# An encoder layer on one core: the gate's SiLU, the gate's load and the first block sums moved

## The chip, the core and the metric

The kernel runs on one core of a Trainium2 chip. The metric is the device time of one execution in microseconds (us); lower is better. The core has a matrix engine (TensorE, in the profile PE, its weight loads PEld), a vector engine (VectorE, DVE), a scalar engine (ScalarE, ACT), a general engine (GpSimd, POOL) and a queue engine (SyncE, SP). Each works through its own instructions strictly in the order in which the program issued them, so an instruction that waits holds up all that stand behind it on its engine. Transfers are issued from SP and POOL and run on 16 DMA engines.

## The reference, cut to what matters

One layer over 512 tokens of width 2048:

```python
h = rmsnorm(x); proj = h @ w_in                      # 2048 x 6176
aq, ak, av, gq, gk, gv, gr, glr = split(proj)
attn_out = mixture_of_dilations(aq, ak, av)          # 16 heads of 64
o = gla(forward) + gla(backward)                     # 4 heads, gated linear attention
gla_out = rmsnorm_per_head(o) * gla_norm_w * silu(gr)
x = x + concat(attn_out, gla_out) @ w_out
h = rmsnorm(x)
x = x + (silu(h @ w_gate) * (h @ w_up)) @ w_down     # hidden width 5632
out = rmsnorm(x)
```

`gr` (width 1024) is the output gate of the gated linear attention ("GLA"): its SiLU is taken early, kept in DRAM, and multiplied in at the end of each GLA head.

## The kernel before

All products work on float32 values split into a rounded part (`hi`, made by ACT) and a remainder (`lo`, made by DVE), and each product is hi x hi + hi x lo + lo x hi. Most large products use a fast scheme with seven instead of eight block products of 2 x 2 blocks; its weight operands are four raw blocks and four sums of them ("block sums", class `Blocks`, `sums`, lines 1394 to 1396), and its results are put together by an evacuation (`evac7`).

The program is written out by hand in one order; there is no planner. These parts matter here.

**The front stage (`Front.run`).** Twelve units of 256 output columns, four weight pieces each: units 0 to 3 are the output gate `gr`, units 4 to 11 are q and k of the windowed attention. For piece i the loop issues the splits and sums of the next pieces (`split(i + 1)`, lines 1407 and 1412; `sums(i + 2)`), then the 14 pairs of products (lines 1489 and 1503), then one call of `run_urgent`, which takes one step of the oldest pending generator. At the last piece of a unit, `evac7` starts: its first step copies and adds the seven PSUM results (lines 1523 and 1529 to 1537). Its second step, one piece later, makes the last add (line 1523, 128 x 512) and issues four accumulating DMAs on POOL (lines 1548 to 1551) that add three partial results into the unit's output tile. Three empty steps follow, the third of which ends in `finish`: DVE multiplies by the row scale (line 1646), and for a gate unit ACT takes SiLU (line 1650) and POOL stores both halves to DRAM (`grd`, line 1651), all in one step. With one step a piece, the multiplication and SiLU of unit u fall at the end of piece 3 of unit u + 1, behind that unit's own first evacuation step.

**Side work.** After the front stage, attention and the four GLA heads run as generators beside the projections. Each half weight piece of a projection earns credit, and each step of side work costs one. `gla(h)` loads its gate (`load_gate`, line 877, issued on POOL) just before the step that transposes the normalized output (line 1093) and multiplies it by the gate (line 1096). Line 966 makes the decayed q and k, line 998 multiplies them on PE; `load_gv` loads the values.

**Block sums made ahead (`Feed.ahead`).** The feed-forward's gate and up projections (`Feed`, 44 units of four pieces) need DVE for block sums. For 21 pieces, those of `pre`, the sums are made earlier, during the projections of the mixed output: raw blocks are loaded by SP, four adds are made in place (line 1463), and POOL stores them to DRAM (`sd`, line 1465). Later `Feed.sums` loads them on SP. The pace is set by `j.ahead`, steps a half piece, for the six projections before the last. The first five pieces' sums are made directly from the raw blocks, in six smaller instructions a piece (`halves=True`), during the last two projections (`before_out`, called at pieces 5, 7, 9, 11 and 13 of their 16 halves). Their splits (line 1412) stand on DVE among the remainders of the projection's own weights (line 218).

## Time and profile before

| | |
|---|---|
| median of three executions | 2179.76 us (2178.83 to 2181.34) |
| the profiled execution | 2178.09 us, span 2176.3 us |
| PE busy | 2156.1 us (99%) |
| DVE busy | 1821.7 us (84%) |
| ACT busy | 1221.7 us (56%) |
| POOL busy | 359.8 us (17%) |
| front stage, row-scale multiplications of its 12 units | 143.9 to 379.4 us |
| block sums made ahead | 624.6 to 821.1 us |
| products of gate and up begin | 850.8 us |

How to read the rows: a row of the timeline has its start, its duration, engine, source line (L1646 is line 1646), operation, the tiles written and read (a and b are the two pools of buffers, ps is PSUM), the shape, and in square brackets how long the engine had stood idle before it and what ended that wait. A row of the view of stretches has the stretch, its length, then the busy time and the number of instructions of PE, PEld, DVE, ACT and POOL, the granted clock of PE as a share of full speed, the busy share of the DMA engines, and GB/s. "DMA to landing" is the time from a DMA's issue to its completion.

### The profile page before, as it was taken

The numbers are of one execution on the slowest core, as the hardware profiler recorded it, in microseconds if no ns is written. First come the engines' busy times: TensorE is split into PE (matmuls) and PEld (weight loads), VectorE is DVE, ScalarE is ACT, GpSimd is POOL, SyncE is SP. The second block draws the span as 40 slices with busy tenths as digits, with TensorE's granted clock in tenths as the row PEclk, the third lists the DMA queues.
The fourth block names the chain that finished last, engine by engine and source line by source line (L and its number), as shares of the span: only waits on it lengthen the run. The fifth ranks groups of instructions, "written<-read, shape, count | busy, mean of one in ns | idle before, by whom it ended". The sixth has DMA issues, their size and how long they took to land.

```text
span 2176.3 us, 34923 instructions
## 1 busy us (share of the span) xinstructions
PE 2156.1 (99%) x12682; PEld 1899.3 (87%) x12682; DVE 1821.7 (84%) x3153; ACT 1221.7 (56%) x2229; POOL 359.8 (17%) x503
## 2 busy tenths in 40 slices
PE   9999999999999999999999999999999999999998
PEld 7888887888887888988888888888888899999987
DVE  6698996777768678899899999998999888898885
ACT  8455554677655445555555555555555655555562
POOL 0012123211011110012211122121221220021300
PEclk9999999999999999999999999999999999999999
DMA  6467779536366773377767677677777985576982
GB/s 201 141 174 173 174 179 251 165 120 187 109 224 212 251 261 117 122 182 178 197 178 182 181 177 196 177 181 184 177 193 174 269 204 173 184 183 156 284 309 78
DMA packets 264475, 405.71 MB, mean 186 GB/s; under 512 B 19373, under 2 KB 163421, under 8 KB 264302
## 3 DMA queue, kind: packets, MB, share of 16 engines
q1 hardware_dynamic: 205502, 272.49, 39.6%
q0 software_dynamic: 58480, 130.45, 26.7%
q8 instruction: 100, 1.64, 0.3%
q14 instruction: 73, 0.60, 0.1%
q10 hardware_dynamic: 320, 0.53, 0.1%
HBM read 287.47 MB, written 66.39 MB: 163 GB/s over the span
## 4 chain that ended last, share of the span: by engine, by line
PE 57%; DVE 0%; DMA 0%; issue 0%; ACT 0%; DVEq 0%; ACTq 0%
PE ps L1503 24%; PE ps L1489 12%; PE ps L1867 5%; PE ps L1868 5%; PE ps L1866 5%; PE ps L348 1%; PE ps L346 1%; PE ps L347 1%; PE ps L2063 1%; PE ps L2061 1%; PE ps L2062 1%; DMA gd<-b 0%; DVE b L1412 0%; DVE a L2094 0%; DVE a L1523 0%
## 5 line engine op out<-in xcount | busy, mean ns | idle before, releaser
L1407 ACT CAST b<-b 128x768 fp32r<-128x768 f32 (+1 forms) x569 | 518.7, 944 | 373.4 <-DVE b L1412 181.7
L1412 DVE TENSOR_TENSOR b<-b,b 128x768 fp32r<-128x768 f32 (+1 forms) x569 | 597.8, 1085 | 36.4 <-ACT b L1407 25.2
L1503 PE MATMUL ps<-b,b 128*128 128x512 f32 x1656 | 484.3, 393 | 0.9 <-ACT b L1407 0.7
L1503 PE MATMUL ps<-a,b 128*128 128x512 f32 x1368 | 401.4, 394 | 2.1 <-DVE b L1523 1.7
L1503 PEld LDWEIGHTS ps<-b,b 128*128 128x128 f32 x1656 | 280.8, 188 | 32.8 <-ACT b L1407 1.5
L1489 PEld LDWEIGHTS ps<-b,b 128*128 128x128 f32 x1656 | 271.3, 190 | 39.3
L1489 PE MATMUL ps<-b,b 128*128 128x256 f32 x1656 | 296.8, 280 | 0.0
L1489 PEld LDWEIGHTS ps<-a,b 128*128 128x128 f32 x1368 | 227.0, 189 | 38.1 <-DVE b L1412 2.1
L1503 PEld LDWEIGHTS ps<-a,b 128*128 128x128 f32 x1368 | 228.0, 189 | 25.6 <-ACT b L1407 2.5
L1489 PE MATMUL ps<-a,b 128*128 128x256 f32 x1368 | 246.0, 281 | 0.5 <-DVE b L1412 0.2
L1394 DVE TENSOR_TENSOR b<-b 128x512 f32<-128x512 f32 x260 | 178.3, 686 | 21.7 <-DMA b<-in_w_down_dram 6.4
L1866 PE MATMUL ps<-b,b 128*128 128x256 f32 x624 | 176.6, 283 | 0.0
L1867 PE MATMUL ps<-b,b 128*128 128x256 f32 x624 | 176.6, 283 | 0.0
L1868 PE MATMUL ps<-b,b 128*128 128x256 f32 x624 | 176.6, 283 | 0.0
L1866 PEld LDWEIGHTS ps<-b,b 128*128 128x128 f32 x624 | 119.8, 192 | 0.0
L1867 PEld LDWEIGHTS ps<-b,b 128*128 128x128 f32 x624 | 119.8, 192 | 0.0
L1868 PEld LDWEIGHTS ps<-b,b 128*128 128x128 f32 x624 | 119.8, 192 | 0.0
L1396 DVE TENSOR_TENSOR b<-b,b 128x256 f32<-128x256 f32 x260 | 110.7, 426 | 8.9
L1395 DVE TENSOR_TENSOR b<-b,b 128x256 f32<-128x256 f32 x260 | 110.5, 425 | 9.0
L346 PE MATMUL ps<-b,b 128*128 128x512 f32 x292 | 117.0, 401 | 0.3 <-ACT b L455 0.3
L348 PE MATMUL ps<-b,b 128*128 128x512 f32 x292 | 114.1, 391 | 0.2 <-DVE b L459 0.2
L347 PE MATMUL ps<-b,b 128*128 128x512 f32 x292 | 113.9, 390 | 0.0
(301 smaller groups left out, 4199.3 us busy)
## 6 DMA issues: line engine op xcount, KB each, us to landing
b<-in_w_gate_dram SPq DMA_DIRECT2D x109, 512.0 KB, 4.0
b<-in_w_up_dram SPq DMA_DIRECT2D x88, 512.0 KB, 4.4
b<-in_w_down_dram SPq DMA_DIRECT2D x88, 512.0 KB, 5.5
b<-a POOLq DMA_DIRECT2D x162, 256.0 KB, 4.6
b<-in_w_in_dram SPq DMA_DIRECT2D x78, 512.0 KB, 3.9
b<-in_w_out_dram SPq DMA_DIRECT2D x32, 512.0 KB, 5.3
gd<-b POOLq DMA_DIRECT2D x22, 512.0 KB, 4.0
b<-gd SPq DMA_DIRECT2D x22, 512.0 KB, 5.5
```

What stands on the lines that cost most here:

```text
L346: mm(o, xh.t[:, c], wh.t[:, w], start=first and not on, stop=False, skip_group_check=on)
L347: mm(o, xh.t[:, c], wl.t[:, w], start=False, stop=False, skip_group_check=on)
L348: mm(o, xl.t[:, c], wh.t[:, w], start=False, stop=last, skip_group_check=on)
L1394: dve.tensor_tensor(s_[:, :, 0:2], r[:, :, 1:3], r[:, :, 0:1].to_broadcast(shape), op=OP.add)
L1396: dve.tensor_tensor(s_[:, :, 3], s_[:, :, 2], r[:, :, 3], op=OP.add)
L1407: act.copy(o, src)
L1412: dve.tensor_tensor(o, src, h, op=OP.subtract)
L1489: mm(o, wl, xh, start=False, stop=end, skip_group_check=True)
L1503: mm(o.rearrange("p (s t) -> p s t", s=2), wh, x_, start=first and p == 0, stop=False, skip_group_check=True)
L1866: mm(o, xh[:, t], wh, start=first and h == 0, stop=False, skip_group_check=True)
L1867: mm(o, xh[:, t], wl, start=False, stop=False, skip_group_check=True)
L1868: mm(o, xl[:, t], wh, start=False, stop=last, skip_group_check=True)
```

## The change

1. **Front stage.** For gate units the generator's last part is cut in two: the multiplication in one step, SiLU and the store (one DMA instead of two) in the next. To make room, `Front.run` calls `run_urgent` twice in piece 0 of units 1 to 4.
2. **GLA.** One step more behind the products of line 966; the gate is loaded behind the first state products instead of just before it is used, and a step stands where the load was.
3. **Block sums.** The first five pieces of gate and up join `pre` (26 instead of 21); their sums are loaded from DRAM as two halves each, at the places where they were computed. The pace of `ahead` rises from 1.25 to 1.5 steps a half piece for the first three projections, from 2.0 to 2.25 for the next two and from 1.0 to 2.25 for the one after them.

```diff
@@ gla(h) @@
             if h % 2 == 0:
                 load_gv(h // 2)
             yield
+            yield
             put(gq.pop(h), gk.pop(h))
...
             sums(0)
+            load_gate(h)
             yield
             decays(0)
             sums(1)
...
             put(*os_)
-            load_gate(h)
+            yield
             yield
@@ Feed.__init__ @@
                 self.pre = {i: n for n, i in enumerate(
-                    i for i, (u, q) in enumerate(seq) if u > 1 and q == 1 and u % 2 == 0)}
+                    i for i, (u, q) in enumerate(seq) if i < 5 or u > 1 and q == 1 and u % 2 == 0)}
@@ Feed.sums @@
                     self.n_sums += 1
-                    S = s4.get(F32, self.shape(4))
-                    self.S[i] = [S]
-                    sp.dma_start(out=S.t.rearrange("p a b c -> p (a b c)"), in_=self.sd[self.pre[i]])
+                    n = 2 if halves else 1
+                    S = [s2.get(F32, [P, 1, 4, P]) for _ in range(2)] if halves else [s4.get(F32, self.shape(4))]
+                    self.S[i] = S
+                    for p, S in enumerate(S):
+                        sp.dma_start(out=S.t.rearrange("p a b c -> p (a b c)"),
+                                     in_=self.sd[self.pre[i]][:, p * 1024 // n:(p + 1) * 1024 // n])
@@ Front.finish @@
                     dve.tensor_tensor(c_.t, c_.t, rb[1].t[:, None, :].to_broadcast([P, 2, 512]), op=OP.mult)
-                    if u < 4:
-                        tables(SILU)
-                        for f in (1, 0):
-                            act.activation(c_.t[:, f], c_.t[:, f], AF.Silu, scale=1.0 - 2.0 * f)
-                            pool.dma_start(out=grd[u][:, f * 512:(f + 1) * 512], in_=c_.t[:, f])
-                    else:
+                    if u >= 4:
                         pool.dma_start(out=qkd[u - 4], in_=c)
+                        put(c_)
+
+                if u < 4:
+                    do()
+                    yield
+                    tables(SILU)
+                    for f in (1, 0):
+                        act.activation(c_.t[:, f], c_.t[:, f], AF.Silu, scale=1.0 - 2.0 * f)
+                    pool.dma_start(out=grd[u], in_=c)
                     put(c_)
-
-                if u == len(self.units) - 1:
+                elif u == len(self.units) - 1:
                     self.late = do
@@ Front.run @@
                     run_urgent()
+                    if q == 0 and 0 < u <= 4:
+                        run_urgent()
                     if done:
                         urgent.append(done)
@@ the order of the jobs @@
-            j.ahead = {n_out: 0.0, n_out - 1: 1.0}.get(n, 2.0 if n_in <= n < n_out else 1.25 if n_in - 3 <= n < n_in else 0.0)
+            j.ahead = {n_out: 0.0, n_in: 2.25}.get(n, 2.25 if n_in < n < n_out else 1.5 if n_in - 3 <= n < n_in else 0.0)
```

More of the change, by code (lines that the diff above doesn't have):

```diff
@@ L2133, in layer @@
             if n == n_out:
-                assert next(state["sums"], None) is None
+                assert next(state["sums"], 0) == 0
                 ff.run()
```

## The prediction

> **What bounds the kernel now.** I read the page first, then the waits, then the places that the waits name.

> ```profile
> PE 2156.1 (99%) x12682; PEld 1899.3 (87%) x12682; DVE 1821.7 (84%) x3153; ACT 1221.7 (56%) x2229; POOL 359.8 (17%) x503
> ```

> TensorE (PE) is busy for 99% of the span, so a change pays only where PE stands still, and costs only where it makes PE stand still. The view of the waits, PE's rows alone, says who keeps it (us in total, times, longest):

> ```profile
> PE ps L347 <- DVE a L218: 2.0, 1, 2.0
> PE ps L1503 <- DVE b L1523: 1.9, 5, 1.0
> PE ps L998 <- DVE a L1096: 1.8, 1, 1.8
> PE ps L1093 <- ACT b L1086: 1.5, 2, 1.1
> PE ps L1503 <- ACT b L1407: 1.1, 5, 0.2
> ```

> Three places, one for each part of the change: the entry to the feed-forward (L347), the front stage with its gate units (L1503), the gated attention (L998, L1093). The edits cannot win more than these stops and the slow clock after them.

> **Part 1, the front stage.** In the timeline of VectorE (DVE), L1523 over 128x512 is the add that opens a unit's last step; right behind it POOL issues that unit's four accumulating DMAs. L1646 is the multiplication by the row scale, which reads what those DMAs wrote.

> ```profile
> 128.23 0.69 DVE L1523 TENSOR_TENSOR b<-b,a 128x512 f32<-128x512 f32 x1
> ...
> 149.43 0.69 DVE L1523 TENSOR_TENSOR b<-b,a 128x512 f32<-128x512 f32 x1
> ...
> 157.08 0.69 DVE L1394 TENSOR_TENSOR b<-b 128x512 f32<-128x512 f32 x1
> ...
> 162.19 0.76 DVE L1523 TENSOR_TENSOR a<-ps,a 128x256 f32<-128x256 f32 x2 [0.19 <-DMA b<-a]
> ...
> 163.65 1.22 DVE L1646 TENSOR_TENSOR b<-b,a 128x1024 f32<-128x1024 f32 x1
> ...
> 166.81 2.18 DVE L1412 TENSOR_TENSOR b<-b,b 128x768 fp32r<-128x768 f32 x2 [0.42 <-ACT b L1407]
> ...
> 168.90 0.69 DVE L1523 TENSOR_TENSOR b<-b,a 128x512 f32<-128x512 f32 x1
> ...
> 171.43 0.69 DVE L1394 TENSOR_TENSOR b<-b 128x512 f32<-128x512 f32 x1 [1.84 <-issue]
> ...
> 190.32 0.69 DVE L1523 TENSOR_TENSOR b<-b,a 128x512 f32<-128x512 f32 x1
> ...
> 211.72 0.69 DVE L1523 TENSOR_TENSOR b<-b,a 128x512 f32<-128x512 f32 x1
> ```

> From add to add one unit passes. 149.43 to 168.90 is 19.47; less the two idle times in it (0.19 and 0.42) DVE needs 18.86. PE needs as much: the stretch of an undisturbed unit without gate is 19.52.

> ```profile
> 248.58:268.10 19.52, 19.52 (x113) 17.14 (x114) 18.26 (x31) 9.96 (x17) 4.07 (x5) 1.00 0.68 162
> ```

> So DVE has 0.7 us to spare in a unit, and the four gate units (128.23 to 211.72, 83.49) run above that. The cause shows on ScalarE (ACT):

> ```profile
> 186.32 1.15 ACT L1650 ACTIVATE b<-b 128x512 f32<-128x512 f32 x2 [3.00 <-DVE b L1646]
> ```

> SiLU waits 3.00 for the multiplication, ACT's roundings behind it come late, the store of the gate comes late, and DVE then waits 1.84 for the buffer that the store reads.

> Now count the steps. Each unit's evacuation is a generator, one step a weight piece; the multiplication is its fifth. Before, the steps fall on the next unit's pieces 0, 1, 2, 3 after the first. The change calls twice in piece 0 for the gate units, so steps two and three fall on piece 0, four on piece 1, the multiplication on piece 2, SiLU on piece 3. SiLU keeps its piece; the multiplication moves one piece forward. In DVE's queue its new place is before the block sums at 157.08, that is 157.08 - 149.43 = 7.65 after the add. Has the data landed by then? POOL's timeline, and the landing times of L1551 and L1549 over the four gate units (min/median/max):

> ```profile
> 136.76 1.20 POOL L1551 DMA_DIRECT2D b<-a  x1
> ...
> 157.78 0.86 POOL L1550 DMA_DIRECT2D b<-a  x1 [5.30 <-DMA b<-a]
> 158.32 1.20 POOL L1551 DMA_DIRECT2D b<-a  x1
> ...
> 177.95 1.21 POOL L1551 DMA_DIRECT2D b<-a  x1
> ...
> 200.00 1.20 POOL L1551 DMA_DIRECT2D b<-a  x1
> ```
> ```profile
> DMA to landing us min/median/max: 3.7/3.8/5.6
> ```
> ```profile
> DMA to landing us min/median/max: 5.6/6.2/6.8
> ```

> No. The third DMA waits for the first two, which overlap it; the fourth is issued 8.53, 8.89, 9.05 and 9.68 after the add, and lands 3.7 to 5.6 later (the four landings sum to 3.7 + 2 x 3.8 + 5.6 = 16.9). The times from add to landing sum to 36.15 + 16.9 = 53.05, on average 13.3 against 7.65. DVE stands about 5.6 us in each unit; queued behind the multiplication are the sums and remainders of the next unit's first piece, then the evacuation that frees PSUM, and PE waits for both. In the old place, 163.65 - 149.43 = 14.2 after the add, the data are there.

> After the landing DVE still has 18.86 - 7.65 = 11.21 of its unit to do. Four units take 53.05 + 4 x 11.21 = 97.9 instead of 83.5: **+14.4**. PE and ACT are no cover: PE finishes the unit in 19.5, within 24. The gains are already in this: the 1.84 and 0.42 are not in the 18.86, and a late gate buffer would be waited for inside the landing time. Ends: with the shortest landing (3.7) four times, 36.15 + 14.8 + 44.84 - 83.49 = +12.3; if PE alone set the pace, 4 x 19.52 - 83.49 = -5.4. I take the sum of the four, measured at this very place, with +18 (another 1 us a unit, the spread of L1549) as upper end. One store of 512 KB for two of 256 KB saves POOL an issue; POOL stands idle behind it, so nothing.

> [...]

> **Part 2, gated attention.** One yield more behind the products with q and k, one more behind the scaling, and the gate's load (L877, POOL) eight steps sooner. PE, timeline:

> ```profile
> 657.67 1.86 PE L1093 MATMUL ps<-idn,b 128*128 128x128 f32 x8 [1.06 <-ACT b L1086]
> 660.06 1.05 PE L998 MATMUL ps<-a,a 128*128 128x128 f32 x8
> ...
> 689.65 1.49 PE L1093 MATMUL ps<-idn,b 128*128 128x128 f32 x8 [0.45 <-ACT b L1086]
> 693.61 0.60 PE L998 MATMUL ps<-a,a 128*128 128x128 f32 x3 [1.77 <-DVE a L1096]
> ```

> Then the idle time that ended at the gate's landing (view of L1096), the gate load's time to landing (view of L877), and the first and last product of L998:

> ```profile
>   DMA b<-grd: 14.6, 3
> ```
> ```profile
> DMA to landing us min/median/max: 6.4/9.2/10.7
> ```
> ```profile
> L998 PE MATMUL ps<-a,a x64: 270/275/377, 629.2 to 721.3; 128*128 128x128 f32 x64
> ```

> Eight 128-wide products take 1.05 when fed. The transposes lose 1.06 + 0.81 and 0.45 + 0.44 because their scaling was issued just ahead of them; a step between them removes that. The 1.77 come from L1096, which stood for the gate, 14.6 us in three waits. The load lands 6.4 to 10.7 after its issue; one head's steps from its first L998 (629.2) to its transposes (657.67) are twelve in 28 us, so eight steps are some 19 us and cover it. Sum **-4.5**; ends -4.5 and +1 (a buffer of 4 KB a partition held 19 us longer, eight steps more of side work for the same credit; DVE, at 31.91 of 50 us in the row below, has room for a later crowd). On POOL the load passes the next head's loads and a store of block sums that waits for DVE; it can at worst stand behind such a store, where it stands today.

> **Part 3, entry to the feed-forward.** Stretches (us, PE, PEld, DVE, ACT, POOL, granted clock), then DVE's timeline:

> ```profile
> 845.00:848.20 3.20, 1.25 (x5) 1.05 (x6) 3.20 (x6) 0.00 (x0) 0.00 (x0) 1.00 0.07 10
> 848.20:851.60 3.40, 3.40 (x11) 2.80 (x10) 3.16 (x6) 1.95 (x6) 1.62 (x3) 0.50 0.67 218
> ```
> ```profile
> 835.23 0.42 DVE L1394 TENSOR_TENSOR a<-b 128x256 f32<-128x256 f32 x1
> ...
> 837.21 0.69 DVE L218 TENSOR_TENSOR a<-b,a 128x512 fp32r<-128x512 f32 x1
> ...
> 846.21 0.69 DVE L218 TENSOR_TENSOR a<-b,a 128x512 fp32r<-128x512 f32 x1
> ```

> PE stands 1.95 for the weight remainder at 846.21, and then runs 3.40 at a clock of 0.50, which costs 1.70. DVE has no gap in this stretch, and one piece's block sums, six instructions, hold it for 1.98 (835.23 to 837.21). Three of the five pieces lie in this last projection, two of them from 835 on: at least 4.0 us leave the queue ahead of a remainder that comes 1.95 late. **-3.65**, ends 0 and -3.65. What would be late next is the same remainder, 2 us later than needed to hurt.

> The price of it: 20 adds made ahead over the six projections before (L1463), which are 20 x 0.42 = 8.4 us of DVE in stretches like this one:

> ```profile
> L1463 DVE TENSOR_TENSOR b<-b x84: 410/419/428, 624.6 to 821.1; 128x256 f32<-128x256 f32 x84
> 700.00:750.00 50.00, 50.00 (x244) 42.26 (x244) 31.91 (x70) 23.82 (x63) 6.40 (x12) 1.00 0.66 220
> ```

> DVE is busy 31.91 of 50 there, so nothing; uncovered, where the rate more than doubles (1.0 to 2.25 a half piece, the last projection but one), it would be 8 adds, 3.4 us, less the two pieces of sums that leave that same projection, 4.0. SP issues five raw loads and ten loads of half sums more, POOL five stores more: 7.9 MB at the 220 GB/s of that row are 36 us of DMA time within 230, beside a share of 0.66. No weight load ends a wait of PE today; I take nothing, with +1 as end.

> **Sum.** 14.4 - 4.5 - 3.65 = **+6.25**. The profiled execution took 2178.09 (span 2176.3 and 1.8 around it), 1.67 under the median of the runs, 2179.76; on the median that is **2186.0**.

> **Rivals.** *Stall, but no gains* (the side steps meet new waits, the sums come late by DMA): 2179.8 + 14.4 = 2194. Against it: three waits with names, each taken apart from its cause. For it: 1.0 to 2.25 crowds DVE. A variant: each PE stop of some 4 us in the front is followed by 3.40 at half clock, as at 848; 4 x 1.70 = 6.8 more, 2193, if PE had no slack. It has: 19.5 + 1.7 against 24.5 a unit.

> *The accumulations land sooner* (other side, not slower). The first two need 5.6 to 6.8 while the last needs 3.7; the gate's store now leaves 3 us earlier and may no longer share the queue with them. It decides where 4 x (L + 11.21) - 83.49 = 8.15, an average L of 11.7 instead of 13.3. If the first two landed in 3.7 too, L = 13.3 - 2.5 = 10.8: front +4.5, total -3.6, 2176. Against it: 128.23 has no store ahead of it, and its L is the longest (8.53 + 5.6).

> *No stall at all* (faster): the data are there 7.65 after the add. Then DVE needs 18.86 and PE's 19.52 sets the pace: front -5.4, total -13.6, 2166. The rows have no L under 12. [...]

> **How the numbers follow.** Forecast 0.67, own range 2182 to 2191; stall without gains 0.10; sooner landings 0.15; no stall 0.08. Two runs of this kernel can be told apart from about 0.2%, 4.4 us: 2175.4 and 2184.1. Of the forecast 0.15 falls below 2184.1, of the sooner landings 0.05 below 2175.4. Slower 0.52 + 0.10 = 0.62, within 0.15 + 0.10 = 0.25, faster 0.05 + 0.08 = 0.13. The range, 2174 to 2194, leaves out the last rival, half of the first and the tails, 0.18.

> **What would show it.** Right: L1646 of the four gate units stands 3 to 6.5 us for a DMA of tile b, adds about 24 apart, PE waits of 2 to 4 us on DVE L1412 or L1523 between 140 and 230; no wait of L1650 for L1646; no idle time of L1096 for the gate; clock 1.00 at 848. Wrong: gate units at 21.4 or less, L1646 without idle time, or the L347 wait still there.

## The result, and the profile after

The changed kernel takes 2199.28 us (2197.20 to 2201.22), beside 2178.83 for the kernel before on the same chip: a ratio of 1.0092, 95% interval 1.0078 to 1.0107. Slower was right; 2186.0 was 13.3 us too low, and the range (2174 to 2194) did not hold the time.

TensorE's waits after the change, line numbers now those of the changed kernel (L1494 and L1508 are the old L1489 and L1503, L1414 the old L1412, L1528 the old L1523, L1284 the old L1282):

```profile
span 2199.5 us, 34945 instructions
PE 2165.2 (98%) x12682; PEld 1907.7 (87%) x12682; DVE 1820.5 (83%) x3143; ACT 1222.5 (56%) x2229; POOL 359.8 (16%) x504
...
PE ps L1494 <- DVE b L1414: 9.9, 5, 3.0
PE ps L1508 <- DVE a L1528: 3.6, 4, 1.0
PE ps L346 <- ACT a L237: 3.1, 1, 3.1
PE ps L1072 <- DVE b L1284: 2.5, 1, 2.5
PE ps L1508 <- DVE b L1528: 1.9, 3, 1.0
PE ps L1024 <- DVE b L1284: 1.6, 1, 1.6
```

The old waits that the prediction named are gone or shorter: L347's fell from 2.0 to 0.4, L998's for the gate and L1093's for the scaling are not there. In their place stand others, one kind for each part. Both kernels issue the same 12682 matmuls, so the delay can be read by number (the two profiled executions lie 23.2 apart, the medians 20.5): the start of the n-th matmul in one trace less that in the other (us, worked out from the two traces, at the matmul that starts nearest to each time of the kernel before).

```
                                        after less before
front stage, up to 206 us                    +20.0
rest of it, up to 234                         -1.0
on to 640 us                                  +0.4
gated attention, 640 to 760                   +1.5
entry to the feed-forward, up to 852          +1.8
after it                                      +0.4
sum (spans: 2199.5 - 2176.3 = 23.2)          +23.1
```

The three parts in turn. **Front stage**, DVE's timeline: the adds that open a unit's last step, and the multiplication (L1651):

```profile
128.13 0.68 DVE L1528 TENSOR_TENSOR b<-b,a 128x512 f32<-128x512 f32 x1
142.16 1.23 DVE L1651 TENSOR_TENSOR b<-b,a 128x1024 f32<-128x1024 f32 x1 [6.29 <-DMA b<-a]
153.34 0.69 DVE L1528 TENSOR_TENSOR b<-b,a 128x512 f32<-128x512 f32 x1
168.04 1.23 DVE L1651 TENSOR_TENSOR b<-b,a 128x1024 f32<-128x1024 f32 x1 [6.96 <-DMA b<-a]
179.22 0.69 DVE L1528 TENSOR_TENSOR b<-b,a 128x512 f32<-128x512 f32 x1
193.13 1.23 DVE L1651 TENSOR_TENSOR b<-b,a 128x1024 f32<-128x1024 f32 x1 [6.17 <-DMA b<-a]
204.31 0.68 DVE L1528 TENSOR_TENSOR b<-b,a 128x512 f32<-128x512 f32 x1
218.48 1.23 DVE L1651 TENSOR_TENSOR b<-b,a 128x1024 f32<-128x1024 f32 x1 [6.42 <-DMA b<-a]
229.66 0.69 DVE L1528 TENSOR_TENSOR b<-b,a 128x512 f32<-128x512 f32 x1
```

The wait is where the prediction put it, but 6.2 to 7.0 instead of 5.6. Four units take 229.66 - 128.13 = 101.5, 18.0 more than before (83.5). From add to multiplication pass 14.03 + 14.70 + 13.91 + 14.17 = 56.8 (forecast 53.05); the rest is 44.7 (forecast 4 x 11.21 = 44.8). The landing of the last accumulating DMA (L1556) over the four gate units, min/median/max:

```profile
DMA to landing us min/median/max: 5.4/5.6/5.8
```

Before it was 3.7/3.8/5.6. Over the four units these landings sum to 22.4, where the forecast had 16.9, so they are 5.5 us longer. The DMA itself was issued 2.2 us earlier in all than the forecast had it, which gave a part of that back.

**Entry to the feed-forward**, ACT's timeline, the landing of the block-sum store that was issued at 835.15, and the stretch behind the stop:

```profile
843.53 1.14 ACT L148 CAST b<-b 128x512 fp32r<-128x512 f32 x2 [7.84 <-issue]
```
```profile
DMA to landing us min/median/max: 8.3/8.3/8.3
```
```profile
846.70:850.00 3.30, 3.30 (x10) 2.57 (x9) 3.27 (x8) 0.54 (x2) 0.76 (x2) 0.53 0.73 226
```

The old stop at 845 is gone, but ACT stands 7.84 in the projection before it, PE then 3.1 (L346 for L237), and the clock behind that is 0.53. The view names no releaser for ACT's wait, but the trace holds it: ACT's wait instruction ahead of that rounding ends at 843.49, and of the two semaphores that it waits for one counts the landing of this store, with the last count at 843.47 (835.15 + 8.3); the other had not changed for 9 us. ACT wanted a buffer that the store was still reading.

### The profile page after: what moved, and what is told of

It reads as the page before. It is cut to its first block, busy times and chain, and to the rows that moved or that the text cites. A ratio compares the mean times of both kernels' runs of the same rounds, so it can differ in the third digit from the quotient of the medians.

```text
span 2199.5 us, 34945 instructions
## 1 busy us (share of the span) xinstructions
PE 2165.2 (98%) x12682; PEld 1907.7 (87%) x12682; DVE 1820.5 (83%) x3143; ACT 1222.5 (56%) x2229; POOL 359.8 (16%) x504
## 4 chain that ended last, share of the span: by engine, by line
PE 57%; DVE 0%; DMA 0%; issue 0%; ACT 0%; DVEq 0%; ACTq 0%
PE ps L1508 24%; PE ps L1494 12%; PE ps L1878 5%; PE ps L1877 5%; PE ps L1876 5%; PE ps L347 1%; PE ps L348 1%; PE ps L346 1%; PE ps L2073 1%; PE ps L2071 1%; PE ps L2072 1%; DMA gd<-b 0%; DVE b L1414 0%; DVE a L2104 0%; DVE a L1528 0%
## 5 line engine op out<-in xcount | busy, mean ns | idle before, releaser
L1414 DVE TENSOR_TENSOR b<-b,b 128x768 fp32r<-128x768 f32 (+1 forms) x569 | 597.6, 1084 | 35.0 <-ACT b L1409 23.3
L1508 PE MATMUL ps<-b,b 128*128 128x512 f32 x1656 | 485.2, 394 | 0.4 <-ACT b L1409 0.2
L1508 PE MATMUL ps<-a,b 128*128 128x512 f32 x1368 | 406.7, 398 | 5.4 <-DVE a L1528 3.6
L1494 PEld LDWEIGHTS ps<-b,b 128*128 128x128 f32 x1656 | 271.7, 190 | 50.2 <-DVE b L1414 11.1
L1508 PEld LDWEIGHTS ps<-b,b 128*128 128x128 f32 x1656 | 281.5, 189 | 32.0 <-ACT b L1409 0.7
L1494 PE MATMUL ps<-b,b 128*128 128x256 f32 x1656 | 297.8, 281 | 9.3 <-DVE b L1414 9.3
L1494 PEld LDWEIGHTS ps<-a,b 128*128 128x128 f32 x1368 | 230.3, 191 | 38.4 <-DVE b L1414 1.0
L1508 PEld LDWEIGHTS ps<-a,b 128*128 128x128 f32 x1368 | 230.7, 191 | 28.9 <-DVE a L1528 4.5
L1494 PE MATMUL ps<-a,b 128*128 128x256 f32 x1368 | 248.0, 283 | 0.5 <-DVE b L1414 0.5
L346 PE MATMUL ps<-b,b 128*128 128x512 f32 x296 | 118.8, 401 | 0.0
L347 PE MATMUL ps<-b,b 128*128 128x512 f32 x296 | 115.5, 390 | 0.0
```

The costliest lines, as they stand in the source:

```text
L346: mm(o, xh.t[:, c], wh.t[:, w], start=first and not on, stop=False, skip_group_check=on)
L347: mm(o, xh.t[:, c], wl.t[:, w], start=False, stop=False, skip_group_check=on)
L1414: dve.tensor_tensor(o, src, h, op=OP.subtract)
L1494: mm(o, wl, xh, start=False, stop=end, skip_group_check=True)
L1508: mm(o.rearrange("p (s t) -> p s t", s=2), wh, x_, start=first and p == 0, stop=False, skip_group_check=True)
```

## The experiments

The parts were taken alone first. "Front", "GLA" and "sums" are the three parts of the change; times beside an experiment are its median, and ratios go to the kernel before on the same chip.

### The front part

The front part alone:

```
 dve.tensor_tensor(c_.t, c_.t, rb[1]..., op=OP.mult)
+yield                       # SiLU and store a step later
 ...
 run_urgent()
+if q == 0 and 0 < u <= 4:
+    run_urgent()
```

> The front part alone (SiLU a step behind the multiplication, two steps in piece 0 of units 1 to 4). Theory A, the moved multiplication waits for the accumulating DMAs: four waits of about 6.3 us on the multiplication, four adds about 25 us apart instead of 21, +18 to +21 us in all, nearly all of what the whole change costs. Rival B, the cost lies in the other two parts or in their meeting: less than +10 us here.

Measured: 2196.89, ratio 1.0083 (1.0068 to 1.0098), +19.0 us.

The same, with one condition altered, so that the multiplication keeps its old place and SiLU goes a piece later:

```
-if q == 0 and 0 < u <= 4:
+if q == 0 and 1 < u <= 5:
```

> The front part alone, but the second call of a step stands in piece 0 of units 2 to 5 instead of 1 to 4: the multiplication keeps its old place (piece 3) and SiLU comes one piece later, as the change's words have it. Theory A, only the place of the multiplication costs: no wait on the multiplication, no wait of SiLU, gate units 19.5 to 20 us apart, -3 to -5 us against the kernel before. Rival B, splitting the step costs by itself (the buffer held a piece longer, the later store of the gate): 0 us or slower.

Measured: 2172.49, ratio 0.9971 (0.9961 to 0.9982), 5.4 us faster than the kernel before. The place of the multiplication, with SiLU one piece behind it in both, is worth 24.4 us, and cutting SiLU off it (with one store in place of two) is a gain in itself. DVE, front part alone and with the old place:

```profile
167.19 1.23 DVE L1646 TENSOR_TENSOR b<-b,a 128x1024 f32<-128x1024 f32 x1 [6.00 <-DMA b<-a]
```
```profile
164.70 1.22 DVE L1646 TENSOR_TENSOR b<-b,a 128x1024 f32<-128x1024 f32 x1
```

In the old place it stands for nothing.

Is it the landing, or the new order? The front part alone, without the last two accumulating DMAs of the gate units:

```
-pool.dma_start(out=c[:, 256:768], in_=r3.t, accum_op=OP.add)
-pool.dma_start(out=c[:, 768:1024], in_=r3.t[:, z], accum_op=OP.add)
+if not (isinstance(self, Front) and u < 4):
+    ... the same two
```

> The front part alone, as changed, but the third and fourth accumulating DMA of the four gate units are left out (a part of the gate's sums is then missing from the output; four DMAs of 256 and four of 128 KB less). Theory A (the multiplication in its new place waits for the landing of the last accumulating DMA): only the first two DMAs are left, the second is issued 1.8 us after the add and lands 5.6 to 6.8 later, 7.4 to 8.6 after the add, where the multiplication's place is 7.65. So it waits 0 to 1 us instead of 6.2 to 7.0, the adds are 19.5 to 20.5 us apart instead of 25.4, PE's stops of 2 to 3 us in 140 to 230 are gone, and the time is 2172 to 2178, 19 to 25 below the front part alone (2196.9). Theory B (the new order of DVE's queue costs by itself, whatever has landed): the adds stay 24 us or more apart, 2190 or more.

Measured: 2173.81, ratio 0.9980 (0.9971 to 0.9989). DVE's multiplication, at the same early place:

```profile
160.00 1.22 DVE L1647 TENSOR_TENSOR b<-b,a 128x1024 f32<-128x1024 f32 x1 [0.36 <-DMA b<-a]
```

It is the only wait of the four multiplications. The time is 1.3 above that with the old place, and by the matmuls' starts only 0.3 of it arises in the gate units. So the early order costs next to nothing by itself; what costs is the wait for those two DMAs. Why they land late is not told by this run, since their bytes are left out with them.

Why do they land later than before? Each piece's weights (512 KB) are loaded by SP when a buffer comes free. The loads next to the last accumulating DMA of the second gate unit, before and after (that DMA is issued at 158.32 before and at 162.20 after):

```profile
156.41 0.37 SPq L1375 DMA_DIRECT2D b<-in_w_in_dram  x1
```
```profile
162.68 0.37 SPq L1377 DMA_DIRECT2D b<-in_w_in_dram  x1
```

1.9 us earlier in the one, 0.5 later in the other. The view of the DMA queues between issue and landing, before and after (packets, MB, share of 16 engines):

```profile
q0 software_dynamic: 288, 0.39, 65.0%
q1 hardware_dynamic: 413, 0.41, 31.5%
```
```profile
q0 software_dynamic: 288, 0.39, 47.0%
q1 hardware_dynamic: 544, 0.54, 30.6%
```

POOL's bytes are the same, and the whole load runs beside them. This was to be shown by moving the load. First the multiplication was called ahead of the next piece's split, which was thought to hold the load back:

```
 self.sums(i + 2)
+if q == 2 and 0 < u <= 4:
+    run_urgent()            # and not at the end of the piece
 self.split(i + 1)
```

> The front part alone, as changed, with the multiplication of the gate units called ahead of the split of the next piece, instead of behind it, in the same weight piece. The split releases the raw weights' buffer, so the load of 512 KB that was issued at 161.75, together with the last accumulating DMA, can then be issued only behind the multiplication. Theory G (that load is what lengthens the landing): the last accumulating DMA of the gate units two to four lands in 3.7 to 4.0 us instead of 5.4 to 6.1, though DVE waits some 6.5 us for it (the split's 2.1 us now stand behind the wait). The time moves little: 8.3 + 3.75 + 11.2 + 2.1 = 25.3 us from add to add against 24.9 in the front part alone, 2196 to 2200. Theory H (the accumulations are slow here for another reason): landing 5.4 or more as before, wait of 8 or more, adds 27 apart, 2203 to 2207.

Measured: 2204.34, one execution. The edit did not hold the load back in three of the four units, and the time is theory H's, with PE stopped up to 5.9 us in a unit. But the units differ, and that tells the theories apart. In the second the load is issued 2.0 before the DMA (167.06); in the third, with it (192.66). The loads and the landings of the two units:

```profile
165.03 0.37 SPq L1375 DMA_DIRECT2D b<-in_w_in_dram  x1
DMA to landing us min/median/max: 3.7/3.7/3.7
```
```profile
192.75 0.37 SPq L1375 DMA_DIRECT2D b<-in_w_in_dram  x1
DMA to landing us min/median/max: 5.5/5.5/5.5
```

Then the number of raw pieces held was altered in those units, which moves every load:

```
+self.most = 2 if 0 < u <= 4 else 3      # and 4 in the second run
 self.load()
```

> The front part alone, as changed (multiplication early), with two raw weight pieces held instead of three in the four units, so that each load of 512 KB is asked for at another moment. Theory G (a load issued together with the last accumulating DMA lengthens its landing): units whose load is issued within 1 us of that DMA land in 5.4 to 6.1 us, units whose load is 2 us or more away from it in 3.7 to 4.0, whichever they are; if all four come free of it, DVE's waits shrink from 6.0 to 6.6 to some 4.3, and the time by up to 4 x 1.9 = 7.5 us, to 2189. Theory H (the landing hangs on the multiplication's new place or on what DVE does meanwhile): 5.4 or more wherever the load lies, 2195 to 2199.

> The same with four raw weight pieces held, one more than in the change, which asks for each load at yet another moment. Theory G: as in the run with two, by the distance of the load from the last accumulating DMA, 3.7 to 4.0 or 5.4 to 6.1; 2189 to 2198 by how many units come free of it. Theory H: 5.4 or more in all four, 2195 to 2199.

Measured: 2189.71 with two, 2194.33 with four, one execution each. Landing of the last accumulating DMA (L1551) of the gate units, with two and with four:

```profile
DMA to landing us min/median/max: 3.7/4.4/4.8
```
```profile
DMA to landing us min/median/max: 3.7/4.3/4.8
```

The multiplication has the change's early place in both, and the landings shrink: theory H, which had 5.4 or more, falls. With two held, DVE's waits are 3.5 to 4.5, and the time is what theory G gave. The two groups of landings that G forecast did not show; with a load 1.5 away, landings of 4.5 lie between them. With four held, the loads met the first two accumulating DMAs in two of the units (L1549 lands in 5.0 to 8.3), in the second unit the last one was issued only 11.2 after the add, and DVE waited 4.1 to 7.5: little was won.

The traces on record carry this further. Here are the gate units of all 15 kernels that have this DMA in them, 60 landings, sorted by how far from the DMA's issue the nearest load was issued (us, worked out from the traces):

```
nearest load                            DMAs    landing
within 0.5                                21    5.4 to 6.1
1.0 to 1.7 before or behind               10    4.2 to 4.9
1.8 or more away                          29    3.7 to 4.3
```

The three groups do not overlap but for a tenth at the last border. All four units of the change are in the first group.

### The attention part

The GLA part alone:

```
 load_gv(h // 2)
 yield
+yield                       # behind the products with q and k
 ...
 sums(0)
+load_gate(h)                # sooner
 yield
 ...
-load_gate(h)
+yield                       # behind the scaling
 yield
```

> The gated attention alone (gate loaded sooner, two steps more a head). Prediction as made: no wait for the gate and none of the transposes for their scaling, -4.5 us. Rival, the steps only shift which products meet the projection's own evacuation: the named waits gone, new ones of the same size (0 to +2 us).

Measured: 2177.94, ratio 0.9997 (0.9987 to 1.0006): nothing. PE's waits between 620 and 760:

```profile
PE ps L1072 <- DVE b L1284: 2.3, 1, 2.3
PE ps L1024 <- DVE b L1284: 1.4, 1, 1.4
PE ps L1072 <- DVE b L1043: 0.3, 1, 0.3
```

The waits for the gate and the scaling are gone as forecast. But the head's products now come just when DVE evacuates a projection's four banks (L1284, four instructions, 2.48 us), and wait for a bank. The first two rows stand in the changed kernel too.

On top of the front part with the multiplication in its old place (2172.49), the sooner load alone:

```
 sums(0)
+load_gate(h)
 yield
 ...
-load_gate(h)
```

> The front part with the multiplication in its old place (2172.5 by the run before), and of the attention part the gate's load alone, issued sooner; no added steps. Theory C (the load pays, the added steps spoil it by meeting the projection's evacuation): the wait of the gate's product for the gate is gone, PE's stop of 2.46 us on it with it, and no stop of a projection's product for the evacuation comes: 1.8 to 4 us less, 2168.5 to 2170.7. Theory D (whatever frees the attention's steps lets them run into the next wait, as with the whole attention part, which came to nothing): 2171.5 to 2174.

Measured: 2172.55, ratio 0.9974 (0.9963 to 0.9985). By the matmuls' starts the attention gains 2.5 us, and 1.6 are lost at the entry, where the clock fell behind the old stop (below). So theory C is right on the waits, while the time is theory D's: nothing was won in it.

Then with the step behind the scaling as well, but not the one behind the products with q and k:

```
-load_gate(h)
+yield
 yield
```

> The front part with the multiplication in its old place, and of the attention part the sooner load and the added step behind the scaling; the added step behind the products with q and k is left out. It tells which step met the evacuation. Theory I (the step behind the products with q and k shifts the later steps into the evacuation; the other is harmless): the transposes' stops of 1.2 and 0.6 are gone with the gate's, no stop over 1.5 us of L1070 or L1023's products on DVE's L1282, 2.5 to 4.5 below 2172.5, 2168 to 2170. Theory D (any shift runs into a next wait): a stop of 1.5 to 2.6 us of such a product for the evacuation comes, 2171.5 to 2174.

Measured: 2167.75, ratio 0.9956 (0.9942 to 0.9969), 4.7 below 2172.49. The two intervals overlap a little, but the slowest of these executions (2169.03) is faster than the fastest of the others (2171.64). PE's waits between 620 and 760 have one row left:

```profile
PE ps L998 <- DVE a L966: 0.2, 1, 0.2
```

Theory I holds: the -4.5 of the prediction is there to be had. What gave it back is, by all that the runs show, the one step behind the products with q and k: the three kernels of the record that have it and the sooner load (this part alone, the whole change, and the change with one condition altered) show the two stops for L1284, and the four that have the sooner load without it show neither. No two runs differ in that step alone.

### The block sums

The sums part alone:

```
-i for i, (u, q) in enumerate(seq) if u > 1 and ...
+i for i, (u, q) in enumerate(seq) if i < 5 or u > 1 and ...
-pace 1.25, 2.0, 1.0
+pace 1.5, 2.25, 2.25
```

> The block sums alone (five pieces more made ahead, faster pace). Prediction as made: the stop in the last projection and the slow clock behind it gone, -3.65 us. Rival, the faster pace makes its own stop in the last projection but one, as the trace of the changed kernel has near 842 us: 0 to +3 us.

Measured: 2184.28, ratio 1.0025 (1.0014 to 1.0035), +6.4 us. ACT in the last projection but one, and the landing of the store issued at 819.75:

```profile
828.00 1.14 ACT L148 CAST b<-b 128x512 fp32r<-128x512 f32 x2 [7.71 <-issue]
```
```profile
DMA to landing us min/median/max: 8.2/8.2/8.2
```

819.75 + 8.2 = 827.95: the changed kernel's stop, with nothing else of the change in place. By the matmuls' starts this entry loses 1.7 net of the old stop that is gone. Another 4.1 are lost in the attention: 1.7 behind the first head's transposes, where the clock fell (0.79 from 660 to 668, 1.00 in the stretch of before), and 2.4 at the old gate wait, which here stands 2.56 (1.77 before) with a slow clock behind it, in this part alone and before:

```profile
697.30:701.00 3.70, 3.53 (x16) 3.24 (x17) 3.70 (x8) 1.69 (x4) 0.54 (x1) 0.60 0.46 108
```
```profile
693.50:697.00 3.50, 3.39 (x21) 3.04 (x22) 3.50 (x8) 2.24 (x4) 0.54 (x1) 1.00 0.71 246
```

In the whole change both of these waits are gone, which accounts for most of the 5 by which the parts' sum (19.0 + 0 + 6.4 = 25.4) is above the whole (2199.28 - 2178.83 = 20.45).

With the old pace of 1.0 in the last projection but one, and a higher one before it, on top of the front part with the multiplication in its old place:

```
-pace 1.5, 2.25, 2.25
+pace 1.85, 2.25, 1.0
```

> The front part with the multiplication in its old place (2172.5), and the early block sums with another pace: 1.0 a half piece in the last projection but one, as before the change, 2.25 in the one before that, 1.85 in the three before. Theory E (the sums' gain at the entry is real, and the loss comes from the crowd in the last projection but one, where ScalarE's rounding stood 7.7 us for the buffer of a store that landed after 8.2): that wait falls under 2 us, no PE stop of 3 us between 810 and 835, and the remainder's stop of 2.15 at the entry is gone as well: 3.8 less than 2172.5, 2168 to 2170. Theory F (five more stores and ten more loads cost wherever they lie): some other stop of 2 to 4 us with half clock behind it comes in their place, 2173 to 2179.

Measured: 2173.85, ratio 0.9982 (0.9973 to 0.9990). PE has no wait between 800 and 880 any more, neither the old nor the new one, and ACT's wait for a buffer now has its releaser's name:

```profile
816.10 0.62 ACT L148 CAST b<-b 128x512 fp32r<-128x512 f32 x1 [3.48 <-DMA sd<-b]
```

The entry gains 2.3 by the matmuls' starts; some 1.8 are lost up to 690, where the pace is now 1.85 beside the attention's steps (that the pace does it is not shown). The store still lands in 7.5 us, but ACT comes for its buffer 4.0 after the issue instead of 0.5, so its wait is 3.48 (theory E had under 2) and stops nothing. The time is not below 2172.49 and lies in theory F's range, without a stop of the size that F expected. So theory E is right on the place and the cause; the gain did not reach the time.

Three pieces made early instead of five, with the sooner gate load:

```
+i < 3 or ...;  pace 1.5, 2.25, 1.0
```

> The front part with the multiplication in its old place, the gate's load sooner without added steps, and the block sums of the first three pieces (not five) made early, with the paces 1.5, 2.25 and, in the last projection but one, 1.0. Theory E (the entry's stop goes, and with a low pace in the last projection but one nothing takes its place): no PE stop over 1 us between 800 and 860 and no half clock there; no stop for the gate: 2 to 6 us below 2172.5, 2166.5 to 2170.5. Theory F (each of these gains is given back by another stop, by the clock or in the transfers): 2171.5 to 2175.

Measured: 2172.17, ratio 0.9977 (0.9969 to 0.9986). PE's wait at the entry is back (L347 for L218, 1.94). The fourth and fifth pieces, left as they were, still have their sums made just ahead of the late remainder:

```profile
828.57 0.42 DVE L1394 TENSOR_TENSOR a<-b 128x256 f32<-128x256 f32 x1
...
835.49 0.42 DVE L1394 TENSOR_TENSOR a<-b 128x256 f32<-128x256 f32 x1
```

The time is theory F's. Three pieces are the wrong three: with all five made early the stop is gone, so it hangs on the last two.

All that held, together: the front part with the multiplication in its old place, the sooner gate load with the step behind the scaling, five pieces with paces of 1.5, 2.6 and 1.0.

> The front part with the multiplication in its old place, the gate's sooner load with the step behind the scaling (together 2167.75), and the early block sums of five pieces with the paces 1.5, 2.6 and, in the last projection but one, 1.0. Theory E (the entry's stop can be had without a new one): no PE stop over 1 us between 800 and 860; 2.2 us less if the clock stayed up behind that stop, 3.9 less if it fell: 2164 to 2166. Theory F (the sums' gain is given back elsewhere): 2167 to 2170.

Measured: 2166.09, ratio 0.9949 (0.9936 to 0.9963). The best of all runs, 12.5 us faster than the kernel before and 33 faster than the change; a tenth above theory E's range. No stop at the entry; the stretch that answers to it:

```profile
834.00:842.00 8.00, 8.00 (x50) 7.14 (x49) 7.36 (x16) 2.81 (x9) 2.16 (x4) 1.00 0.55 185
```

What the sums add to 0.9956 lies within the intervals; in the trace it is 2.2 us at the entry, beside 1.7 that this profiled run had lost by 256.

### The whole change with one condition altered

```
-if q == 0 and 0 < u <= 4:
+if q == 0 and 1 < u <= 5:
```

> The whole change with one condition altered: the second step call in the units after the first gate unit's, so that the multiplication keeps its old place. If the parts add up: the change's time less what that place cost in the front part alone (24.4 us), 2199.3 - 24.4 = 2174.9; from the parts' own runs, -5.4 + 0 + 6.4 on 2177.9, 2178.9. Theory A (the place of the multiplication is the whole loss of the change): 2172 to 2179. If the other two parts held a loss of their own that the front's stall only hid: above 2182.

Measured: 2176.95, ratio 0.9995 (0.9986 to 1.0004). With the multiplication in its old place the change is as fast as the kernel before, so that place is all of its net loss. But the front part in the same place ran at 2172.49: the other two parts together still cost 4.5 us here. Their waits are those of the change (L1072 and L1024 for L1284, 2.5 and 1.6; L346 behind ACT's rounding, 3.3).

## Why the prediction was wrong, point by point

In the trace of the whole change the three terms came out 4.6, 6.0 and 5.5 us above the forecast (+19.0, +1.5 and +1.8), so no single one is the miss.

**Front, +14.4: the mechanism right, the term too small.** Measured +19.0 alone. The failed step is "I take the sum of the four, measured at this very place": the landings of before (3.7 to 3.9 in three of the four) were measured with the multiplication in the other place, where the weight load came 1.9 to 2.9 us ahead of the last accumulating DMA. In the change it came within 0.5 of it, and the landings were 5.4 to 5.8. The row that fitted was there: the one gate unit with 5.6, whose load was issued 0.14 behind the DMA, and the same DMA in the feed-forward of the kernel before, 40 times:

```profile
DMA to landing us min/median/max: 3.7/5.6/7.7
```

With 5.6 for all four the term is 36.15 + 22.4 + 44.84 - 83.49 = 19.9, near the measured 19.0 (18.0 from add to add). The upper end of 18 was too low for the same reason. The remainder of 11.21 a unit held (44.7 in four).

**GLA, -4.5: the gain exists, the forecast of no price was wrong.** The failed step is "DVE ... has room for a later crowd", with +1 as the end. The price was not DVE's load but one instant: a head's products meeting the four-instruction evacuation. Each of two added steps was costed as harmless; with one of them in, all that the other edits won was gone (2177.94 alone, nothing; 4.7 won in the run without it).

**Sums, -3.65: the gain exists, the price was looked for in the wrong place.** The old stop went, as forecast. The failed step is "No weight load ends a wait of PE today; I take nothing, with +1 as end". What came was a wait of ACT for a buffer that a late store still read, 7.7 us, in the projection whose pace rose most, and PE's 3.1 behind it. Measured alone, +6.4; the trace puts 1.7 net of it at the entry and 4.1 in the attention.

**Rivals.** "Stall, but no gains" came nearest (2194, given 0.10); the change took 5 more, the landings' share. "The accumulations land sooner" was half right: the first two did (5.4/5.5/6.0 after 5.6/6.2/6.8), but the last one, which the multiplication waits for, landed later. "No stall at all" had the data there 7.65 after the add; the multiplication, which waits for them, came 13.91 to 14.70 after it, and the last landing alone took 5.4 to 5.8.

**The signs to look for.** Right: the place of L1651's wait, the adds about 25 apart (24 forecast), PE waits of 2 to 3 on L1414, SiLU's wait down from 3.0 to 0.3, no wait for the gate, the L347 wait down to 0.4. Wrong: L1651's longest wait, 6.96 where 6.5 was the end; clock 1.00 at 848, which is 0.53, behind the new stop.

## What to carry to other kernels

A DMA's time is no constant of the DMA (in the gate units here the same 128 KB landed in 3.7 to 6.1 us): take it from rows where the same other transfers run beside it, and ask where those will lie after the change. A step added to hand-ordered side work moves every later step: look at what it then meets, the four-instruction evacuations first. Where a buffer goes from a store to the next user, the store's landing time is part of that user's wait (here 8.3 us of landing and 7.84 of wait): ask how long behind the issue the user comes. And a stop of about 2 us is best priced twice, with half clock behind it and without (here 3.8 and 2.2 us).

## What the runs showed of the hardware

**A load beside an accumulating DMA.** In the gate units of these kernels the same 128 KB accumulation, issued on POOL behind one of 256 KB, landed in 3.7 to 4.3 us when the nearest load of 512 KB from SP was issued 1.8 us or more away, and in 5.4 to 6.1 when it was issued within 0.5 (60 landings, above). In the second gate unit of the changed kernel the trace has 0.39 MB of POOL's transfers and 0.54 MB of SP's within the same 5.8 us; in what order they were served is not shown.

**The same stop, with and without a slow clock.** PE's stop at the entry is the same in the kernel before and in seven of the experiments (L347 for L218, 1.9 to 2.0 us). The stretch of 3.7 us behind it in the kernel before, and in the front part with the multiplication in its old place:

```profile
847.80:851.50 3.70, 3.70 (x13) 3.03 (x12) 3.46 (x6) 1.90 (x6) 1.52 (x3) 0.56 0.65 200
```
```profile
843.80:847.50 3.70, 3.70 (x26) 3.38 (x25) 3.70 (x7) 2.01 (x7) 1.62 (x3) 1.00 0.63 210
```

13 matmuls against 26. In the stretch of 3.7 us behind the stop the clock was 0.54 to 0.58 in four of the eight (the kernel before, the front part alone, the GLA part alone, the sooner load) and 1.00 in three (the multiplication in its old place, the run without the last two DMAs, the step behind the scaling); in the eighth, with three pieces made early, a matmul of 128x512 took 0.63 us from 1.3 us behind it on, and 0.39 ahead of it. By the matmuls' starts the stop costs 2.2 us, and 1.6 more where the clock falls, so a gain of 2 us elsewhere can vanish in it (as with the sooner load alone).
